# A hybrid SSD and GLA decoder layer: the SSD output kept feature-major, other first loads, and the last norm's shift made on TensorE

## The chip, the cores and the metric

The kernel runs on one core of a Trainium2 chip. TensorE multiplies matrices out of SBUF into PSUM; VectorE (DVE) and ScalarE (ACT) read and write both memories; GpSimd (POOL) works on SBUF alone; loads and stores are issued from the queues of SyncE (SP) and ScalarE. The metric is the device time of one execution in microseconds, less being better.

## The reference

One layer for 256 tokens of width 2048, all in float32:

```
proj = x @ w_in                      # z, xbc, dt, q, k, v, g, lr and two merge gates
xbc  = silu(conv4(xbc))              # gives xs, B, C
y    = ssd(xs, softplus(dt), B, C)   # chunks of 128 tokens, 64 heads of 64, 8 groups, state 128
y    = group_rms_norm((y + D * xs) * silu(z)) * ssd_norm_w    # 8 groups of 512 features
o    = rms_norm(gla(q, k, v, log_sigmoid(lr @ gk_w + gk_b) / 16)) * silu(g)
mix  = (sig(gate_s) * (y @ w_ssd) + sig(gate_g) * (o @ w_gla)) @ w_out
h    = layer_norm(alpha * x + mix)
out  = layer_norm(alpha * h + relu(h @ w_up)^2 @ w_down)
```

Inside a chunk the SSD is a masked product, `y_diag = (C B^T * decay) (x dt)`. For the second chunk a carried-in part is added, `exp(a_cs) * (C prev)`, where `prev` is the state that the first chunk leaves and `a_cs` the running sum of `dt * A`.

## The kernel before

All weights come as one stream of units of 128 x 2048 (1 MB), in the order that `weight_plan` writes out by hand. `Stream` loads each unit on SP's queue into one of three raw buffers and splits it by halves of 1024 columns into a rounded part `whi` (a cast on ScalarE, L139) and a remainder `wlo` (a subtraction on VectorE, L140). Three such halves are kept. Activations are split the same way, so that three products of the fast float32 type stand for one of full precision.

There are two ways to multiply. Form A (`a_unit`, L272 to L288, called by `mm_a`) keeps the activations in the array and moves 512 weight columns: three products (L285 to L287) for each of 16 k-tiles and two token tiles, 96 for a block of 512 features, with tokens on the partitions of the result. Form B (`mm_b`, L245 to L271) keeps the weights in the array and moves the activations: a product of 512 columns (L261) and one of 256 (L264) for each k-tile, 16 such pairs for 128 features, with features on the partitions; a copy (L268) and an addition (L269) then make the sum.

After each half of a unit `run_side` lets a generator go on by a few steps. This is how work that is not the stream of products (scans, norms, the small products of SSD and GLA) gets in between; a planner of the framework then sets the final order on each engine.

The order of stages is: GLA heads 0 to 3, GLA's gates and branch, eight SSD groups, SSD's gates and branch, `w_out`, first norm, `w_up` and `w_down`, last norm. In an SSD group six form-B blocks give xs, B and C with the convolution, then a form-A block gives z, tokens on the partitions. The generator `side_ssd` transposes xs (L670), builds the decayed mask `M` for each chunk, multiplies (L711, features on the partitions), copies, transposes back to token-major (L718), adds the `D` part `yD` and, for the second chunk, the carried-in part (L702 and two passes on VectorE). After z it multiplies, sums squares on ScalarE, takes the power -1/2 on GpSimd for one number a token (`rstd_of`, L328), scales, and transposes again (L740) into the split, feature-major operand of the branch.

At the start ten products of ones (L198) keep TensorE busy, the constants `K` and two small tensors go out on ScalarE's queue, and x and the first weights on SP's. The first side product is `lrT` by `gkw_sb` (L485), with 16 rows. At the end `ln2_last` (L970) norms the second token tile: after the last product VectorE adds, takes statistics, GpSimd takes the power, and VectorE, ScalarE and GpSimd share four blocks of 512 columns.

Of the kernel before, what the change touches and what calls it, by code (L numbers as in the profile page):

```python
# [11 lines left out]
F32 = mybir.dt.float32  # L12
# [25 lines left out]
def weight_plan():  # L38
# [47 lines left out]
class Stream:  # L86
# [26 lines left out]
    def start(self, between):  # L113

        t = self.raw_pool.tile([P, 2048], F32, name="wr", tag="wr")
        for i in range(4):
            q = slice(i * 512, (i + 1) * 512)
            self.nc.sync.dma_start(t[:, q], self.ws[0, :, q])
            between(i)
        self.raws.append(t)  # L120
        self.n_raw = 1
        self._load()
        self._load()
# [48 lines left out]
def hybrid_layer(ctx, tc, ws, xT, x, cst, gkw, dpar, lnp, out):  # L172
# [24 lines left out]
    for _ in range(10):  # L197
        PE.matmul(ps0[:, 0:P], warm, warm, start=True, stop=True)  # L198
# [73 lines left out]
    def a_unit(ps, mat, row, col, u, act, steps=STEPS, units=4):  # L272

        st.expect("A", mat, row + u * 512, col)
        for s in range(2):
            hi, lo = st.half()
            hi = hi.rearrange("p (k c) -> p k c", k=2)
            lo = lo.rearrange("p (k c) -> p k c", k=2)
            for k in range(2):
                kt = u * 4 + s * 2 + k  # L280
                a = act(kt)
                ah, al = a[:, 0], a[:, 1]
                for t in range(2):
                    tt = slice(t * P, (t + 1) * P)
                    pe().matmul(ps[t], ah[:, tt], hi[:, k], start=kt == 0, stop=False)  # L285
                    pe().matmul(ps[t], ah[:, tt], lo[:, k], start=False, stop=False)  # L286
                    pe().matmul(ps[t], al[:, tt], hi[:, k], start=False, stop=kt == 4 * units - 1)  # L287
            run_side(steps)  # L288
# [34 lines left out]

    def rstd_of(pool, ss, scale):
        v = pool.tile([P, 1], F32, name="rv", tag="rv", bufs=2)
        r = pool.tile([P, 1], F32, name="rr", tag="rr", bufs=2)
        V.tensor_scalar(v, ss, scale, EPS, ALU.mult, ALU.add)
        G.tensor_tensor(r, v, nhalf, ALU.pow)  # L328
        return r
# [50 lines left out]
    tokp = cp.tile([P, 6, 64], F32, name="tokp")  # L380

    def side_dt(dtT, pool):
# [33 lines left out]
        S.activation(s2[:, P:T], e[:, P:T], AF.Exp)  # L416
# [3 lines left out]
        for i, src in enumerate((y[:, 0:P], y[:, P:T], e[:, 0:P], e[:, P:T], s2[:, 0:P], s2[:, P:T])):  # L420
            pe().transpose(ps[:, i * 64:(i + 1) * 64], src, ident[0:64, 0:64])
        S.copy(tokp, ps[:, 0:384].rearrange("p (a b) -> p a b", a=6))
# [10 lines left out]
    with tc.tile_pool(name="gla", bufs=1) as gp:  # L433
        ga_scope = ExitStack()
        ga = ga_scope.enter_context(tc.tile_pool(name="gla_in", bufs=1, side="right"))
        gkw_sb = ga.tile([16, 1024], F32, name="gkw_sb")
        lrT = ga.tile([16, T], F32, name="lrT")
# [8 lines left out]
        def load_x(*parts):  # L446
            for i in parts:
                xr[i] = xp.tile([P, 2, T], F32, name="xr", tag="xr", bufs=4)
                nc.sync.dma_start(xr[i], xT[:, 2 * i:2 * i + 2])

        def split_x(i):
            d = xs[:, 2 * i:2 * i + 2]
            S.copy(d[:, :, 0], xr[i])
            V.tensor_tensor(d[:, :, 1], xr[i], d[:, :, 0].bitcast(F32), ALU.subtract)

        def side_x():
            for i in range(2, 8):
                split_x(i)
                if i < 6:
                    load_x(i + 2)  # L460
                yield

        load_x(0)
        st.before[2] = lambda: load_x(2, 3)
        st.start(lambda i: load_x(1) if i == 1 else None)
        split_x(0)
        st.split_first(0)
        st.split_first(1)
# [3 lines left out]
        nc.scalar.dma_start(K, cst)  # L472
        nc.scalar.dma_start(Dbc, dpar.broadcast_to([P, 64]))
        nc.scalar.dma_start(gkw_sb, gkw)
# [100 lines left out]
        for h in range(NH):  # L575
            if h == 0:
                psv, psg = [mtile(), mtile()], [mtile(), mtile()]
                for u in range(4):
                    a_unit(psv, "w_in", 0, C_V, u, xact)
                    a_unit(psg, "w_in", 0, C_G, u, xact)  # L580
                    if u == 1:
                        ps = mm_b("S", "w_in", 0, [xact], bank=stile)
                        S.activation(dtT, ps[0:64], AF.Identity, bias=kcol(K_DTB, 64))
                        S.copy(lrT, ps[64:80])
# [54 lines left out]
    def side_ssd(g, u, sz, yt, ready):  # L639
# [24 lines left out]
        ys = []  # L664
        prev = sp.tile([P, 512], F32, name="prev")
        for c in range(2):
# [7 lines left out]
            yD = sp.tile([P, 8, 64], F32, name="yD", bufs=2)  # L674
            V.tensor_tensor(xdt, psh, hb(tokp[:, c]), ALU.mult)
            if c == 0:
                xw = sp.tile([P, 8, 64], F32, name="xw", tag="xw")
                V.tensor_tensor(xw, psh, hb(tokp[:, 4]), ALU.mult)
            yield
            V.tensor_tensor(yD, psh, hb(Dbc), ALU.mult)  # L680
# [9 lines left out]
            yield  # L690
            for q in range(2):
# [3 lines left out]
            if c == 0:  # L695
                ps = stile()
                pe().matmul(ps, Bt, xw.rearrange("p h e -> p (h e)"), start=True, stop=True)  # L697
                S.copy(prev, ps)
                yield
            else:  # L700
                ps = stile()
                pe().matmul(ps, CT[:, cc], prev, start=True, stop=True)  # L702
                yo = sp.tile([P, 8, 64], F32, name="yo", tag="xw")
                V.tensor_tensor(yo, ps.rearrange("p (h e) -> p h e", h=8), hb(tokp[:, 5]), ALU.mult)
                V.tensor_tensor(yD, yD, yo, ALU.add)
                yield

            py = stile()
            for h in range(8):
                e = h % 2 * 64  # L710
                pe().matmul(py[e:e + 64, h // 2 * P:(h // 2 + 1) * P], xdt[:, h], M[:, h], start=True, stop=True)  # L711
            yield
            yT = sp.tile([P, 512], F32, name="yT", tag="xw")
            S.copy(yT, py)
            yield
            py = stile()
            for i in range(4):
                pe().transpose(py[:, i * P:(i + 1) * P], yT[:, i * P:(i + 1) * P], ident)  # L718
            yield
            yf = yD.rearrange("p h e -> p (h e)")  # L720
            V.tensor_tensor(yf, yf, py, ALU.add)
            ys.append(yf)
# [3 lines left out]
        for c in range(2):  # L726
            y = ys[c]
            V.tensor_tensor(y, y, sz[:, c], ALU.mult)
            ss = sp.tile([P, 1], F32, name="sss", bufs=2)
            S.activation(sz[:, c], y, AF.Square, accum_out=ss)  # L730
            r = rstd_of(sp, ss, 1.0 / 512.0)
            S.activation(y, y, AF.Copy, scale=r)
            yield
        for v2 in range(2):
            ps = stile()
            for j in range(2):
                for c in range(2):
                    f = (v2 * 2 + j) * P
                    o = j * T + c * P
                    pe().transpose(ps[:, o:o + P], ys[c][:, f:f + P], ident)  # L740
            yield
            for j in range(2):
                f = v2 * 2 + j
                w = kcol(K_SN + g * 4 + f)
                pj = ps[:, j * T:(j + 1) * T]
                S.activation(yt[:, f, 0], pj, AF.Copy, scale=w)
                V.scalar_tensor_tensor(yt[:, f, 1], pj, w, yt[:, f, 0].bitcast(F32), ALU.mult, ALU.subtract)
                yield

    ytiles = []  # L750
    for g in range(NG):
# [12 lines left out]
        sz = sp.tile([P, 2, 512], F32, name="sz")  # L764
# [61 lines left out]
    def aggregate(stats):  # L826
        mv = lp.tile([P, 2], F32, name="mv", tag="mv", bufs=2)
        V.bn_aggr(mv, stats)
        r = rstd_of(lp, mv[:, 1:2], 1.0)
        nm = lp.tile([P, 1], F32, name="nm", tag="nm", bufs=2)  # L830
# [139 lines left out]
    def ln2_last():  # L970
        mv, r, nm = aggregate(stats2[:, 1])
        sh = [lq.tile([P, 512], F32, name=f"sh{n}") for n in range(3)]

        def blk(n):
            return (acc[:, 1, n * 512:(n + 1) * 512], gb2[:, 0, n * 512:(n + 1) * 512],
                    gb2[:, 1, n * 512:(n + 1) * 512])

        a0, g0, b0 = blk(0)
        a1, g1, b1 = blk(1)
        a2, g2, b2 = blk(2)  # L980
        a3, g3, b3 = blk(3)
        S.activation(sh[1], g1, AF.Copy, scale=nm)
        S.activation(a3, a3, AF.Identity, scale=r, bias=nm)
        S.activation(a2, a2, AF.Copy, scale=r)
        G.tensor_tensor(sh[1], sh[1], b1, ALU.add)
        G.tensor_tensor(a3, a3, g3, ALU.mult)
        V.scalar_tensor_tensor(sh[0], g0, nm, b0, ALU.mult, ALU.add)
        V.scalar_tensor_tensor(a0, a0, r, sh[0], ALU.mult, ALU.add)
        out_dma(1, 0)
        V.scalar_tensor_tensor(sh[2], g2, nm, b2, ALU.mult, ALU.add)  # L990
        V.tensor_tensor(a2, a2, sh[2], ALU.add)
        out_dma(1, 2)
        V.scalar_tensor_tensor(a1, a1, r, sh[1], ALU.mult, ALU.add)
        out_dma(1, 1)
        V.tensor_tensor(a3, a3, b3, ALU.add)
        out_dma(1, 3)
# [78 lines left out]
```

## Time and profile before

| | |
|---|---|
| median of 3 runs | 2065.91 us (2064.96 to 2067.52) |
| profiled execution | 2071.1 us, its span 2069.4 us |
| TensorE busy | 2052.5 us, 99% |
| VectorE busy | 1272.8 us, 62% |
| ScalarE busy | 1042.0 us, 50% |
| GpSimd busy | 25.5 us, 1% |
| mean granted TensorE clock | 0.995 |
| read from HBM | 391.40 MB, 191 GB/s with what is written |

Busy time says which engine is nearly always occupied, not which wait ends last. The chain goes back from the last instruction and names at each step what released it; windows give the busy time and the granted clock in a stretch. A pass of a full-precision product shows as an instruction of its own, two for each product; a transpose is one.

### The profile page before, as it was taken

To read this page: it belongs to the slowest core of one execution; us is meant where nothing else is said; L and a number is where in the kernel's file an instruction comes from. 1 tells how busy PE (TensorE), PEld (TensorE's weight loads), DVE (VectorE), ACT (ScalarE), POOL (GpSimd) and SP (SyncE) were. 2 spreads that over 40 slices of the span, in tenths; PEclk is the share of its full clock that TensorE was granted. 3 is DMA by queue.
4 is the path that set the end of the run, shared out by engine and by line. 5 is a ranking of instruction groups with operands and counts; after the bars stand their busy time and mean duration, and the time that the engine had idled before them with its cause. 6 is when DMAs were issued, how large, how long until landed. Compare 5 with 4: busy or idle time off the path is not lost.

```text
span 2069.4 us, 25710 instructions
## 1 busy us (share of the span) xinstructions
PE 2052.5 (99%) x10243; PEld 1715.9 (83%) x10243; DVE 1272.8 (62%) x1695; ACT 1042.0 (50%) x1347; POOL 25.5 (1%) x52
## 2 busy tenths in 40 slices
PE   9999999999999999999999999999999999999997
PEld 7888888888888888888888888888888888888886
DVE  5645556445778777777554555686655565565456
ACT  5655545444666666666544443464443443444333
POOL 0000000000000000000000000000000000000000
PEclk9999999999999999999999999999999999999999
DMA  6444455656455554454555556565555555555553
GB/s 249 164 168 168 178 183 214 218 199 223 163 193 194 183 183 177 173 197 167 190 207 198 200 197 224 209 239 185 195 190 190 196 184 198 187 191 195 187 199 122
DMA packets 59321, 397.35 MB, mean 192 GB/s; under 512 B 6736, under 2 KB 6960, under 8 KB 12608
## 3 DMA queue, kind: packets, MB, share of 16 engines
q1 hardware_dynamic: 53568, 374.37, 50.2%
q10 hardware_dynamic: 5632, 21.33, 2.8%
q8 instruction: 80, 1.31, 0.3%
q14 instruction: 41, 0.34, 0.0%
HBM read 391.40 MB, written 4.28 MB: 191 GB/s over the span
## 4 chain that ended last, share of the span: by engine, by line
PE 98%; DVE 1%; DMA 1%; ACT 0%; issue 0%; POOL 0%; DVEq 0%; SPq 0%; POOLq 0%; ACTq 0%
PE mm L261 22%; PE mm L285 19%; PE mm L286 19%; PE mm L287 19%; PE mm L264 11%; PE mm L318 1%; PE sd L711 1%; PE mm L316 1%; PE mm L317 1%; DMA wr<-in_ws_dram 0%; PE sd L718 0%; PE sd L740 0%; PE sd L670 0%; PE sd L697 0%; PE sd L534 0%; PE sd L702 0%
## 5 line engine op out<-in xcount | busy, mean ns | idle before, releaser
L140 DVE TENSOR_TENSOR wlo<-wr,whi 128x1024 fp32r<-128x1024 f32 (+1 forms) x684 | 834.8, 1221 | 660.4 <-ACT whi L139 659.4
L139 ACT CAST whi<-wr 128x1024 fp32r<-128x1024 f32 (+1 forms) x684 | 717.4, 1049 | 887.3 <-PE mm L287 582.1
L261 PE MATMUL mm<-act,whi 128*128 128x512 f32 x1984 | 667.3, 396 | 0.0
L264 PE MATMUL mm<-act,wlo 128*128 128x256 f32 x1984 | 507.4, 280 | 0.0
L261 PEld LDWEIGHTS mm<-act,whi 128*128 128x128 f32 x1984 | 365.8, 188 | 79.2 <-issue 3.4
L264 PEld LDWEIGHTS mm<-act,wlo 128*128 128x128 f32 x1984 | 360.5, 189 | 8.5
L285 PE MATMUL mm<-whi,ys 128*128 128x512 f32 x864 | 336.3, 389 | 0.0
L287 PE MATMUL mm<-whi,ys 128*128 128x512 f32 x864 | 336.2, 389 | 0.0
L286 PE MATMUL mm<-wlo,ys 128*128 128x512 f32 x864 | 336.1, 389 | 0.0
L285 PE MATMUL mm<-whi,act 128*128 128x512 f32 x768 | 312.9, 408 | 0.8 <-ACT whi L139 0.8
L286 PE MATMUL mm<-wlo,act 128*128 128x512 f32 x768 | 301.8, 393 | 1.0 <-DVE wlo L140 1.0
L287 PE MATMUL mm<-whi,act 128*128 128x512 f32 x768 | 301.5, 393 | 0.0
L287 PEld LDWEIGHTS mm<-whi,ys 128*128 128x128 f32 x864 | 162.2, 188 | 33.9
L285 PEld LDWEIGHTS mm<-whi,ys 128*128 128x128 f32 x864 | 162.2, 188 | 33.6
L286 PEld LDWEIGHTS mm<-wlo,ys 128*128 128x128 f32 x864 | 162.2, 188 | 33.5
L285 PEld LDWEIGHTS mm<-whi,act 128*128 128x128 f32 x768 | 145.3, 189 | 37.3 <-issue 6.4
L286 PEld LDWEIGHTS mm<-wlo,act 128*128 128x128 f32 x768 | 145.3, 189 | 34.8 <-issue 2.9
L287 PEld LDWEIGHTS mm<-whi,act 128*128 128x128 f32 x768 | 145.2, 189 | 31.1
L759 DVE SCALAR_TENSOR_TENSOR u<-bsum,K,u 128x255 f32<-128x255 f32 x144 | 68.9, 479 | 26.1 <-ACT u L757 24.9
L269 DVE TENSOR_TENSOR bsum<-mm,bsum 128x256 f32<-128x256 f32 x124 | 51.8, 417 | 12.2 <-ACT bsum L268 12.2
L268 ACT COPY bsum<-mm 128x256 f32<-128x256 f32 x124 | 45.2, 365 | 6.3 <-PE mm L264 6.3
L757 ACT ACTIVATE u<-bsum,K 128x256 f32<-128x256 f32 x48 | 28.9, 601 | 21.8 <-DVE bsum L269 21.8
(230 smaller groups left out, 1246.1 us busy)
## 6 DMA issues: line engine op xcount, KB each, us to landing
wr<-in_ws_dram SPq DMA_DIRECT2D x352, 1024.0 KB, 4.8
abc<-acs_dram ACTq DMA_DIRECT2D x8, 1024.0 KB, 6.7
xr<-in_xT_dram SPq DMA_DIRECT2D x8, 256.0 KB, 6.6
gbias<-gb_dram ACTq DMA_DIRECT2D x8, 256.0 KB, 4.4
mg_dram<-sgr ACTq DMA_DIRECT2D x4, 512.0 KB, 5.9
mgl<-mg_dram ACTq DMA_DIRECT2D x4, 512.0 KB, 3.6
acc<-in_x_dram ACTq DMA_DIRECT2D x2, 1024.0 KB, 7.7
gb<-in_lnp_dram ACTq DMA_DIRECT2D x8, 256.0 KB, 4.6
```

Source lines behind the costliest of these rows:

```text
L139: self.nc.scalar.copy(hi, raw)
L140: self.nc.vector.tensor_tensor(lo, raw, hi.bitcast(F32), ALU.subtract)
L261: PE.matmul(ps, hi[:, k], act(s * 8 + k).rearrange("p s t -> p (s t)"), start=r == 0 and s == 0 and k == 0, stop=False)
L264: PE.matmul(ps[:, T:], lo[:, k], act(s * 8 + k)[:, 0], start=False, stop=r == n - 1 and s == 1 and k == 7)
L268: S.copy(y, ps[:, T:])
L269: V.tensor_tensor(y, ps[:, 0:T], y, ALU.add)
L285: pe().matmul(ps[t], ah[:, tt], hi[:, k], start=kt == 0, stop=False)
L286: pe().matmul(ps[t], ah[:, tt], lo[:, k], start=False, stop=False)
L287: pe().matmul(ps[t], al[:, tt], hi[:, k], start=False, stop=kt == 4 * units - 1)
L316: pe().matmul(ps, ah[:, tt], hi[:, k], start=kt == 0, stop=False)
L757: S.activation(u[:, i], ps, AF.Identity, scale=kcol(K_CW + ft * 4 + 3), bias=kcol(K_CB + ft))
L759: V.scalar_tensor_tensor(u[:, i, j:T], ps[:, 0:T - j], kcol(K_CW + ft * 4 + 3 - j), u[:, i, j:T], ALU.mult, ALU.add)
```

## The change

The block z of each SSD group becomes four form-B blocks of 128 features, so that `silu(z)` has features on the partitions. The SSD output stays feature-major. `yT` takes `D * xs` from the convolved xs and the products from PSUM in one VectorE step for each 128 x 128 piece, with `D` as a column (`Dcol`). The carried-in part is added in PSUM: C is multiplied by `exp(a_cs)` for each head (`abc`), and eight products with `prev` as the array's operand go onto the same PSUM columns. The norm's sum over 512 features is three additions on VectorE and a product with the tile of ones `warm`, which puts each token's sum on all partitions; GpSimd then takes the power of 128 x 256 numbers, and VectorE multiplies. Transposes L718 and L740 are gone.

Besides this: the first loads have other sizes and another order, three warm-up products fewer are made, and the first unit's products with `wlo` come last for each k-tile; the small tensors are loaded behind part 2 of x. `gkw_sb` and `lrT` have 128 partitions of which 112 are zero. In the last norm the shift of three blocks is made in PSUM, `ident` by beta ahead of the statistics and the diagonal of `nm` by gamma behind them, and GpSimd no longer takes part in the blocks.

```diff
-        plan += [("A", "w_in", 512 * i, C_Z + g * 512) for i in range(4)]
+        plan += [("B", "w_in", 0, C_Z + g * 512 + i * P) for i in range(4)]
...
+        for n, cuts in ((0, (0, 512, 1024, 2048)), (1, (0, 1024, 2048))):
+            t = self.raw_pool.tile([P, 2048], F32, name="wr", tag="wr")
+            for a, b in zip(cuts, cuts[1:]):
+                self.nc.sync.dma_start(t[:, a:b], self.ws[n, :, a:b])
+                between(n, a)
+            self.raws.append(t)
...
-    for _ in range(10):
+    for _ in range(7):
...
-        gkw_sb = ga.tile([16, 1024], F32, name="gkw_sb")
-        lrT = ga.tile([16, T], F32, name="lrT")
+        gkw_sb = ga.tile([P, 1024], F32, name="gkw_sb")
+        lrT = ga.tile([P, T], F32, name="lrT")
...
+                if i == 2:
+                    for small, src in ((K, cst), (gkw_sb[0:16], gkw), (Dbc, dpar.broadcast_to([P, 64]))):
+                        G.tensor_copy(small[0:1, 0:1], xr[i][0:1, 0, 0:1])
+                        nc.scalar.dma_start(small, src)
...
+        G.memset(gkw_sb, 0.0)
+        G.memset(lrT, 0.0)
+        nc.scalar.dma_start(xr[0][:, 0], xT[:, 0])
+        def between(n, a):
+            if n == 0 and a == 0:
+                nc.sync.dma_start(xr[0][:, 1], xT[:, 1])
+            elif n == 0 and a == 512:
+                load_x(nc.sync, 1)
+        st.before[3] = lambda: load_x(nc.sync, 2, 3)
+        st.before[4] = lambda: load_x(nc.sync, 4, 5)
+        st.before[5] = lambda: load_x(nc.sync, 6, 7)
...
-            V.tensor_tensor(yD, psh, hb(Dbc), ALU.mult)
...
+                S.activation(abc[:, :, cc], abc[:, :, cc], AF.Exp)
+                V.tensor_tensor(abc[:, :, cc], abc[:, :, cc], CT[:, None, cc].broadcast_to([P, 8, P]), ALU.mult)
...
+            for f in range(4):
+                fc = slice(f * P, (f + 1) * P)
+                for h in (2 * f, 2 * f + 1):
+                    e = slice(h % 2 * 64, h % 2 * 64 + 64)
+                    pe().matmul(py[e, fc], xdt[:, h], M[:, h], start=True, stop=c == 0)
+                if c == 1:
+                    for h in (2 * f, 2 * f + 1):
+                        e = slice(h % 2 * 64, h % 2 * 64 + 64)
+                        pe().matmul(py[e, fc], prev[:, h * 64:(h + 1) * 64], abc[:, h, cc], start=False, stop=True)
+            yield
+            for f in range(4):
+                V.scalar_tensor_tensor(yT[:, f, cc], u[:, f, cc], Dcol[:, g * 4 + f:g * 4 + f + 1],
+                                       py[:, f * P:(f + 1) * P], ALU.mult, ALU.add)
...
+        V.tensor_tensor(yT, yT, sz, ALU.mult)
+        S.activation(sz, yT, AF.Square)
+        yield
+        V.tensor_tensor(sz[:, 0:2], sz[:, 0:2], sz[:, 2:4], ALU.add)
+        V.tensor_tensor(sz[:, 0], sz[:, 0], sz[:, 1], ALU.add)
+        yield
+        yield
+        ps = stile()
+        pe().matmul(ps[:, 0:T], warm, sz[:, 0], start=True, stop=True)
+        v = sz[:, 1]
+        V.tensor_scalar(v, ps[:, 0:T], 1.0 / 512.0, EPS, ALU.mult, ALU.add)
+        G.tensor_tensor(v, v, nhalf.broadcast_to([P, T]), ALU.pow)
+        yield
+        yield
+        V.tensor_tensor(yT, yT, v[:, None, :].broadcast_to([P, 4, T]), ALU.mult)
...
-        ps = mm_a("w_in", 0, C_Z + g * 512, xact)
-        for t in range(2):
-            S.activation(sz[:, t], ps[t], AF.Silu)
+        for i in range(4):
+            ps = mm_b("B", "w_in", C_Z + g * 512 + i * P, [xact])
+            S.activation(sz[:, i], ps, AF.Silu)
...
+        shift = [stile() for n in range(3)]
+        for n in range(3):
+            pe().matmul(shift[n], ident, gb2[:, 1, n * 512:(n + 1) * 512], start=True, stop=False)
+        mv, r, nm = aggregate(
+            stats2[:, 1],
+            lambda: V.tensor_tensor(acc[:, 1, 1536:2048], acc[:, 1, 1536:2048], gb2[:, 0, 1536:2048], ALU.mult))
+        dnm = lq.tile([P, P], F32, name="dnm")
+        S.activation(dnm, ident, AF.Copy, scale=nm)
+        for n in range(3):
+            pe().matmul(shift[n], dnm, gb2[:, 0, n * 512:(n + 1) * 512], start=False, stop=True)
+        sh = lq.tile([P, 512], F32, name="sh")
+        V.scalar_tensor_tensor(sh, gb2[:, 0, 1536:2048], nm, gb2[:, 1, 1536:2048], ALU.mult, ALU.add)
+        for n in (3, 0, 1, 2):
+            a = acc[:, 1, n * 512:(n + 1) * 512]
+            V.scalar_tensor_tensor(a, a, r, sh if n == 3 else shift[n], ALU.mult, ALU.add)
+            out_dma(1, n)
```

## Rows read from the trace of the kernel before

**Rows 1.** The page's chain that ended last, shares of the span by engine.
```profile
PE 98%; DVE 1%; DMA 1%; ACT 0%; issue 0%; POOL 0%; DVEq 0%; SPq 0%; POOLq 0%; ACTq 0%
```
**Rows 2.** Windows, one SSD group: stretch, length, busy time (instructions) by engine, clock, DMA.
```profile
542.60:605.70 63.10, 63.10 (x355) 52.89 (x357) 48.27 (x82) 41.68 (x58) 1.10 (x2) 1.00 0.48 183
```
**Rows 3.** Timeline of TensorE at the start: start, duration, instruction; first and 49th product.
```profile
5.80 1.01 PE L285 MATMUL mm<-whi,act 128*128 128x512 f32 x2
...
20.55 0.39 PE L285 MATMUL mm<-whi,act 128*128 128x512 f32 x1
```
**Rows 4.** Timeline of the tail, from the last product on.
```profile
2056.22 0.39 PE L318 MATMUL mm<-act,ys 128*128 128x512 f32 x1
...
2058.72 0.55 POOL L328 TENSOR_TENSOR rr<-rv,nhalf 128x1 f32<-128x1 f32 x1 [10.33 <-DVE rv L327]
...
2060.16 0.75 DVE L990 SCALAR_TENSOR_TENSOR sh<-gb,nm 128x512 f32<-128x512 f32 x1
...
2060.71 1.32 POOL L985 TENSOR_TENSOR sh<-sh,gb 128x512 f32<-128x512 f32 x1 [1.45 <-ACT sh L982]
2060.82 1.75 DVE L988 SCALAR_TENSOR_TENSOR acc<-acc,rr,sh 128x512 f32<-128x512 f32 x1
...
2064.83 0.68 DVE L995 TENSOR_TENSOR acc<-acc,gb 128x512 f32<-128x512 f32 x1
```
**Rows 5.** Windows around the L485 products; the third last column is the granted clock.
```profile
40.00:44.00 4.00, 4.00 (x16) 2.41 (x15) 2.10 (x4) 3.92 (x9) 0.00 (x0) 1.00 0.07 31
44.00:48.00 4.00, 4.00 (x10) 2.27 (x8) 2.96 (x4) 2.67 (x5) 0.00 (x0) 0.50 0.75 266
...
52.00:56.00 4.00, 4.00 (x10) 3.15 (x10) 0.00 (x0) 2.16 (x5) 0.00 (x0) 0.50 0.02 4
56.00:60.00 4.00, 4.00 (x16) 3.22 (x15) 1.98 (x3) 3.97 (x6) 0.00 (x0) 0.80 0.29 45
```
**Rows 6.** Chain of waits, same stretch: start, time on the chain, engine, tile, line.
```profile
42.54 1.05 PE sd L485 x4
...
48.84 0.43 PE mm L286
```
**Rows 7.** Chain of waits in one SSD group: shares by line, and pieces.
```profile
by line: PE mm L261 35.6%; PE mm L264 18.1%; PE mm L285 11.9%; PE mm L287 11.6%; PE mm L286 11.6%; PE sd L711 3.6%; PE sd L740 1.4%; PE sd L718 1.4%; PE sd L670 1.4%; PE sd L702 1.4%; PE sd L697 1.4%; PE sd L651 1.0%; PE sd L652 0.2%
...
558.62 0.86 PE sd L702 x2
...
562.28 1.02 PE sd L711 x16
563.30 1.12 PE mm L261 x4
...
566.30 0.44 PE sd L718 x4
```
**Rows 8.** Timeline of TensorE, first and last of 68 undisturbed form-B pairs.
```profile
493.43 0.40 PE L261 MATMUL mm<-act,whi 128*128 128x512 f32 x1
...
516.66 0.39 PE L261 MATMUL mm<-act,whi 128*128 128x512 f32 x1
```
**Rows 9.** Groups by line: shapes, count, busy us, mean ns, idle before and releasers.
```profile
L140 DVE TENSOR_TENSOR wlo<-wr,whi 128x1024 fp32r<-128x1024 f32 (+1 forms) x684 | 834.8, 1221 | 660.4 <-ACT whi L139 659.4
L139 ACT CAST whi<-wr 128x1024 fp32r<-128x1024 f32 (+1 forms) x684 | 717.4, 1049 | 887.3 <-PE mm L287 582.1 <-PE mm L261 188.7 <-issue 97.3
...
L269 DVE TENSOR_TENSOR bsum<-mm,bsum 128x256 f32<-128x256 f32 x124 | 51.8, 417 | 12.2 <-ACT bsum L268 12.2
...
L721 DVE TENSOR_TENSOR yD<-yD,sd 128x512 f32<-128x512 f32 x16 | 11.0, 689 | 8.3 <-PE sd L718 8.3
```
**Rows 10.** Cores: span and mean granted clock.
```profile
core 0: 2069.4 us, clock 0.995
```
**Rows 11.** Timeline of ScalarE at the start: casts that waited for weights.
```profile
5.13 0.62 ACT L139 CAST whi<-wr 128x512 fp32r<-128x512 f32 x1 [0.38 <-DMA wr<-in_ws_dram]
...
13.07 1.05 ACT L139 CAST whi<-wr 128x1024 fp32r<-128x1024 f32 x1 [1.78 <-DMA wr<-in_ws_dram]
```

More of the change, by code (lines that the diff above doesn't have):

```diff
@@ L113, in start @@
     def start(self, between):
[L115 to L122, printed above, removed]
+        for n, cuts in ((0, (0, 512, 1024, 2048)), (1, (0, 1024, 2048))):
[4 more added lines that the diff above has]
+            self.raws.append(t)
+        self.n_raw = 2
         self._load()
@@ L282, in a_unit @@
                 ah, al = a[:, 0], a[:, 1]
+                first, last = kt == 0, kt == 4 * units - 1
+                tt = [slice(t * P, (t + 1) * P) for t in range(2)]
+                if st.pos == 1:
+                    for t in range(2):
+                        pe().matmul(ps[t], ah[:, tt[t]], hi[:, k], start=first, stop=False)
+                    for t in range(2):
+                        pe().matmul(ps[t], al[:, tt[t]], hi[:, k], start=False, stop=False)
+                    for t in range(2):
+                        pe().matmul(ps[t], ah[:, tt[t]], lo[:, k], start=False, stop=last)
+                    continue
                 for t in range(2):
[L284 to L287, printed above, removed]
+                    pe().matmul(ps[t], ah[:, tt[t]], hi[:, k], start=first, stop=False)
+                    pe().matmul(ps[t], ah[:, tt[t]], lo[:, k], start=False, stop=False)
+                    pe().matmul(ps[t], al[:, tt[t]], hi[:, k], start=False, stop=last)
             run_side(steps)
@@ L419, in side_dt @@
         ps = stile()
-        for i, src in enumerate((y[:, 0:P], y[:, P:T], e[:, 0:P], e[:, P:T], s2[:, 0:P], s2[:, P:T])):
+        for i, src in enumerate((y[:, 0:P], y[:, P:T], e[:, 0:P], e[:, P:T], s2[:, 0:P])):
             pe().transpose(ps[:, i * 64:(i + 1) * 64], src, ident[0:64, 0:64])
-        S.copy(tokp, ps[:, 0:384].rearrange("p (a b) -> p a b", a=6))
+        S.copy(tokp, ps[:, 0:320].rearrange("p (a b) -> p a b", a=5))
+        Dpair = Dbc.rearrange("p (i two) -> p i two", two=2)
+        G.tensor_copy(Dcol[0:64], Dpair[0:64, :, 0])
+        G.tensor_copy(Dcol[64:P], Dpair[64:P, :, 1])
         yield
@@ L690, in side_ssd @@
             yield
+            if c == 0:
+                ps = stile()
+                pe().matmul(ps, Bt, xw.rearrange("p h e -> p (h e)"), start=True, stop=True)
+                S.copy(prev, ps)
+            else:
+                S.activation(abc[:, :, cc], abc[:, :, cc], AF.Exp)
+                V.tensor_tensor(abc[:, :, cc], abc[:, :, cc], CT[:, None, cc].broadcast_to([P, 8, P]), ALU.mult)
+            yield
             for q in range(2):
@@ L725, in side_ssd @@
             yield "blocked"
[L726 to L747, printed above, removed]
+        V.tensor_tensor(yT, yT, sz, ALU.mult)
[4 more added lines that the diff above has]
+        yield
+        yield
+        ps = stile()
+        pe().matmul(ps[:, 0:T], warm, sz[:, 0], start=True, stop=True)
+        v = sz[:, 1]
+        V.tensor_scalar(v, ps[:, 0:T], 1.0 / 512.0, EPS, ALU.mult, ALU.add)
+        G.tensor_tensor(v, v, nhalf.broadcast_to([P, T]), ALU.pow)
+        yield
+        yield
+        V.tensor_tensor(yT, yT, v[:, None, :].broadcast_to([P, 4, T]), ALU.mult)
+        yield
+        for f in range(4):
+            w = kcol(K_SN + g * 4 + f)
+            S.activation(yt[:, f, 0], yT[:, f], AF.Copy, scale=w)
+            V.scalar_tensor_tensor(yt[:, f, 1], yT[:, f], w, yt[:, f, 0].bitcast(F32), ALU.mult, ALU.subtract)
+            if f % 2:
                 yield
@@ L829, in aggregate @@
         r = rstd_of(lp, mv[:, 1:2], 1.0)
+        with tc.issue_after(var_ins[-1].ins):
+            meanwhile()
         nm = lp.tile([P, 1], F32, name="nm", tag="nm", bufs=2)
```

92 lines of the change are left out of this document (19 added, 73 removed).

## The prediction

> **What bounds the kernel now.** I read the page's chain first: TensorE makes 98% of it [rows 1], so a microsecond counts only where TensorE gains or loses it. Then I looked for the places where that fails. In the SSD stage it never does: one group takes 63.10 us with TensorE busy in all of it, VectorE in 48.27 and ScalarE in 41.68 [rows 2]. At the start the timeline shows the first real product at 5.80 and the 49th at 20.55 [rows 3]; 48 at the 0.231 of a form-A product further on (22.15 us for 96, below) would be 11.1 us, so 3.7 us are waits for loads. At the end the last product starts at 2056.22 and VectorE's last step at 2064.83 [rows 4]: nothing covers that tail. The fourth place is hidden inside a busy TensorE: the granted clock is 1.00 up to 44, 0.50 (1.2 instead of 2.4 GHz) from 44 to 56 and 0.80 in 56 to 60 [rows 5]. TensorE was not idle before it fell; it ran the L485 products, whose operands have 16 partitions, at 1.05 us a pair at the full clock. At the lower level a 512-column product takes 0.43 [rows 6].
>
> **The profiled execution** took 2071.1 us, 1.7 more than its span, and 5.2 more than the median 2065.91. The sum is made against it and carried to the median.
>
> **1. z in form B, eight groups.** The columns are equal: 96 products of 512 before, 64 pairs of 512 and 256 after. In one group's chain the form-A lines hold 35.1% of 63.10, 22.15 us, and the 96 form-B pairs hold 53.7%, 33.88, so 0.353 a pair [rows 7]. 64 pairs are 22.59: 0.44 dearer. From below, the undisturbed stretch at 493.43 to 516.66, 67 pairs, has 0.347 [rows 8]: 0.04 dearer. From above, four more restarts such as the 1.12 instead of 0.93 after a burst [rows 7] make it 1.2.
>
> **2. The SSD output, same groups.** Going: the carried-in product L702 (0.86) and four sets of transposes (L718 and L740, twice each, 0.44 a set): 2.62. Coming: a second burst like L711 for the carried-in part (1.02) and the product with ones, 256 columns of full precision, half of L702: 0.43 [rows 7]. Net 1.17 less. Upper price: a burst's 16 products run 0.064 apart, a transpose of the same 128 columns 0.11; if the interleaving of carried-in and local products ends the overlap of the two column halves, the 32 cost 3.5 instead of 2.04, 1.5 more. From below, the burst could overlap no better than now. With point 1: 0.73 less a group, **5.8 us** over eight (bounds 9.0 less and 12 more).
>
> This costs other engines. VectorE loses eight passes of 128x512 at 0.69 and two tiny ones, 5.8; it gains four sums for z at 0.42, eight steps on 128x128 of PSUM at no more than 0.42, three passes of 1024 columns at 1.22, and 0.69, 0.42 and 0.42 for the norm [rows 9]: 10.2. That makes 52.7 of some 62.4 us, 84%. ScalarE's removed copies, squares and scalings are about what the four extra sums' copies, the wide Exp and Square cost; I take nothing. Both are covered by the weight buffers: a half's cast starts when TensorE frees the buffer (that is the releaser of most casts), the half is due two halves later, 2 x 8 x 0.353 = 5.65 us, and cast and subtraction need 1.05 + 1.22 [rows 9]. So each may come **3.4 us** late for nothing; after that each microsecond is TensorE's. The product with ones waits for two sums on VectorE, with all products queued behind it; the empty turns put around it are worth about a half (2.8 us), more than the 1.1 of the sums.
>
> **3. The power on GpSimd, now 128x256 instead of 128x1.** No row shows it. The one-element form takes 0.55 and a plain 512-column pass 1.32 [rows 4], which gives 0.55 + 0.66 = 1.2 from below; 256 times 0.55 is 141 us from above. It is nearest to the plain pass with the one-element form as its start, so I take 1.2, hidden; it stays hidden while an element costs under 11 ns, four times the plain one. It is not free to VectorE: in the tail L988, 0.75 by itself (L990), took 1.75 beside L985 on GpSimd and ended 0.54 after it; so VectorE stood until GpSimd was done. The subtraction of the weights, two inputs from SBUF like these, is what would stand, and its scaling pass waits for the power as well. The Trainium skill (SBUF — State Buffer, Who interferes with whom) says that "A DVE instruction with two SBUF inputs contends with a GpSimd instruction that reads SBUF", whichever came second waiting for all of the other; the trace agrees. By that rule the whole power falls on VectorE, which is the first rival below.
>
> **4. The 16-partition operands padded to 128.** The low clock lasts 12 + 0.4 x 4 = 13.6 us [rows 5], half of it lost: **6.8 us** less if the wider products hold the clock. Columns and passes stay the same. From below the gain is 0, if zeros count as little as missing rows. I take the full value because the mean clock of 0.995 over 2069.4 us leaves 10.3 us lost [rows 10]: 6.8 here, and the rest falls in the last 8 us, after the products. So nothing else lost the clock, neither the bursts with 64-column operands nor the transposes, and all of those have 128 partitions. The Trainium skill (TensorE: Matmul & The Clock Gate, What's actually happening) sets the clock by how busy the array has lately been. TensorE shows no idle time here, so by busy time alone the padding would do nothing and the sum would be 10.3 less.
>
> **5. First loads.** Before the first cast at 5.13 the constants (350 columns, 0.18 MB), x's part 0 (0.26) and a quarter of a weight unit (0.26) had to land, 0.70 MB; before the cast at 13.07 it was 2.90 MB (all three small loads, two parts of x, two units) [rows 11]: 0.277 MB a us. Now 0.39 MB stand before the first product (1.1 us earlier), and 2.10 before the second unit's first half (2.9 earlier). The second sets the 49th product: **2.9 us** less. Bounds: 0 if x parts 2 and 3, now behind the third unit on SP's queue, are late instead (casts of the next weights would stand behind theirs on ScalarE); 4.8 if all 3.7 of waits go too. The three small loads are issued from ScalarE after x part 2, behind a GpSimd copy; about 1.1 us of issue in front of casts with 3.4 to spare, for constants first used near 40. Three fewer warm-up products: the real ones come before the ten would have ended. The zero fills on GpSimd end before anyone reads.
>
> **6. Tail.** To the power's start, 2058.72, nothing changes [rows 4]. The scaling of the last block (0.69) now stands on VectorE from about 2058.55, so the power waits until 2059.25 and nm is there at 2060.0; then 0.75 for sh and 0.74 for the first block. ScalarE makes the diagonal by about 2060.5; three full-precision products at 0.86 follow, so the blocks end at 2062.25, 2063.05 and 2063.95 instead of 2065.51: **1.6 us** less. The three products with ident go before, 2.6 us from 2056.6, beside VectorE's statistics. Bounds: 2.3 less if the power isn't held up; 0.9 more if the clock falls first (1.72 a product).
>
> Sum: 5.8 + 6.8 + 2.9 + 1.6 = 17.1 less: 2054.0 profiled, **2048.8 us** for the median. With its own bounds this case spans some 2042 to 2055.
>
> **Rivals.**
> *The power holds VectorE* (slower). Place: once a group, beside the weight subtraction. At X us it costs (X - 3.4) x 8. It eats the whole gain at X = 5.5 and is slower by over 0.2% from 6.1; X = 8 gives 2086. For it: the lock is in the trace, and one element at 0.55 is dear. Against: nothing shows how it scales. 0.10 for X between 3.4 and 5.5 (2049 to 2066), 0.14 for more.
> *The padding does nothing* (this part fails to do what it says): 2055.6. For it: TensorE was busy when the clock fell, and the added rows are zeros. Against: point 4. 0.15.
> *The bursts lose their overlap*: 1.5 x 8 = 12 more, 2060.8. Against: local products already alternate the halves. 0.06.
>
> **Chances and range.** The forecast has 0.55. What this kernel's runs can tell from no change is about 0.2%, 4.1 us. Faster (under 2061.8): 0.55 + 0.15 + 0.03 of the third rival + 0.08 of the first = 0.81; same 0.05; slower 0.14. The range 2041 to 2062 reaches from the lower bounds of points 2, 5 and 6 taken in part up to the third rival; outside lie the long powers and a little of the rest, 0.2.
>
> **What would show it.** Right: a group's period of 62.4 with no TensorE gaps; granted clock 1.00 from 40 to 60; the 49th product at 17.7; VectorE's last step about 7.3 after the last product's end. The power's own row on GpSimd decides most: under 3.4 us the subtraction never shows as what TensorE waited for. Wrong: rows of VectorE's subtraction as releasers of TensorE in each group, a pair price above 0.36, or the lower clock again after the L485 products.

## The result, and the profile after

The changed kernel takes 2369.53 us (median of 4, 2368.4 to 2370.62) against 2065.73 of the kernel before on the same chip: 1.1464 times as long, with a 95% interval of 1.1447 to 1.1481. I had forecast 2048.8. The profiled execution spans 2367.7 us.

The page of the kernel after, TensorE's and GpSimd's share, the chain of waits by engine, and the group of the new power:

```profile
PE 2062.5 (87%) x10504; PEld 1738.1 (73%) x10504; DVE 1294.6 (55%) x1760; ACT 1017.6 (43%) x1331; POOL 345.7 (15%) x49
...
PE 83%; POOL 14%; DVE 1%; issue 1%; ACT 0%; DMA 0%; SPq 0%; POOLq 0%; ACTq 0%
...
L765 POOL TENSOR_TENSOR sz<-sz,nhalf 128x256 f32<-128x256 f32 x8 | 329.0, 41122 | 662.2 <-DVE sz L764 662.2
```

TensorE had 98% of the chain before [rows 1]; now GpSimd has 14% of it. The power of 128x256 takes 41.12 us, where I had put 1.2, eight times: 329.0 us. That is near the whole loss of 303.8, but time on GpSimd counts only where TensorE ends up waiting for it. The list of waits says how it reaches TensorE (engine and line that waited, on what, us in total, times, longest):

```profile
DVE yT L768 <- POOL sz L765: 314.8, 8, 41.3
...
PE mm L264 <- DVE wlo L140: 258.6, 7, 37.0
PE mm L295 <- DVE wlo L140: 37.4, 1, 37.4
```

Read upward: TensorE stands 258.6 + 37.4 = 296.0 us for a remainder `wlo` of the weights, and VectorE, which makes `wlo`, stands for the power. VectorE's timeline around the first power, which GpSimd runs from 556.84 to 597.98 (start, duration, instruction, idle before and releaser):

```profile
556.53 0.41 DVE L269 TENSOR_TENSOR bsum<-mm,bsum 128x256 f32<-128x256 f32 x1
556.87 1.67 DVE L140 TENSOR_TENSOR wlo<-wr,whi 128x1024 fp32r<-128x1024 f32 x1
558.46 0.47 DVE L786 SCALAR_TENSOR_TENSOR u<-bsum,K,u 128x255 f32<-128x255 f32 x1
598.01 1.22 DVE L768 TENSOR_TENSOR yT<-yT,sz 128x1024 f32<-128x1024 f32 x1 [39.09 <-POOL sz L765]
599.16 0.48 DVE L786 SCALAR_TENSOR_TENSOR u<-bsum,K,u 128x254 f32<-128x254 f32 x1
599.55 1.22 DVE L140 TENSOR_TENSOR wlo<-wr,whi 128x1024 fp32r<-128x1024 f32 x1
```

One subtraction and one step of the convolution still run beside the power. Then the scaling pass L768, which needs the power's result, is next in VectorE's queue, and the next subtraction stands behind it. TensorE uses up the halves that were split already and stops. The windows show this and what follows it (length, busy time of the engines in the order PE, PEld, DVE, ACT, POOL, granted clock, DMA share, GB/s):

```profile
560.00:596.00 36.00, 3.81 (x22) 3.08 (x21) 0.00 (x0) 0.00 (x0) 36.00 (x1) 0.62 0.00 0
596.00:600.00 4.00, 0.00 (x0) 0.00 (x0) 1.99 (x3) 0.73 (x2) 1.98 (x1) 0.50 0.00 0
600.00:604.00 4.00, 3.18 (x10) 2.79 (x11) 4.00 (x8) 3.72 (x7) 0.00 (x0) 0.50 0.51 178
604.00:608.00 4.00, 4.00 (x18) 3.38 (x18) 3.83 (x9) 2.25 (x4) 0.00 (x0) 0.73 0.62 193
```

TensorE works for the first 3.81 us of the stretch from 560 to 596; after that only GpSimd does. After the idle stretch TensorE comes back at the lower level (0.50) and is at the full one from 608 on, so each group loses a few microseconds more than the wait.

The other parts can be read from the same trace. Around the products of `lrT` the clock is 1.00 in each window, where it was 0.50 [rows 5]:

```profile
44.00:48.00 4.00, 4.00 (x19) 3.11 (x18) 3.80 (x9) 4.00 (x10) 0.00 (x0) 1.00 0.37 156
...
52.00:56.00 4.00, 4.00 (x19) 3.33 (x18) 4.00 (x7) 3.98 (x6) 0.00 (x0) 1.00 0.50 205
```

TensorE's timeline at the start, and at the end TensorE's last product, GpSimd's last power and VectorE's last steps:

```profile
5.65 1.22 PE L287 MATMUL mm<-whi,act 128*128 128x512 f32 x2 [1.17 <-ACT whi L139]
6.67 1.06 PE L289 MATMUL mm<-whi,act 128*128 128x512 f32 x2
...
18.77 0.39 PE L294 MATMUL mm<-whi,act 128*128 128x512 f32 x1
```
```profile
2356.57 0.39 PE L327 MATMUL mm<-act,ys 128*128 128x512 f32 x1
...
2359.07 0.84 POOL L339 TENSOR_TENSOR rr<-rv,nhalf 128x1 f32<-128x1 f32 x1 [10.33 <-DVE rv L338]
...
2361.75 2.46 DVE L1016 SCALAR_TENSOR_TENSOR acc<-acc,rr,sd 128x512 f32<-128x512 f32 x3
```

The 49th product starts at 18.77 (20.55 before [rows 3]; predicted 17.7). The last product of the stream ends at 2356.96, so VectorE's last step ends 7.2 behind it; predicted 7.3, before 8.9 [rows 4].

### The profile page after: what moved, and what is told of

Read it like the earlier page. It is cut to its first block, busy times and chain, and to the rows that moved or that the text cites. A ratio compares the mean times of both kernels' runs of the same rounds, so it can differ in the third digit from the quotient of the medians.

```text
span 2367.7 us, 26328 instructions
## 1 busy us (share of the span) xinstructions
PE 2062.5 (87%) x10504; PEld 1738.1 (73%) x10504; DVE 1294.6 (55%) x1760; ACT 1017.6 (43%) x1331; POOL 345.7 (15%) x49
## 4 chain that ended last, share of the span: by engine, by line
PE 83%; POOL 14%; DVE 1%; issue 1%; ACT 0%; DMA 0%; SPq 0%; POOLq 0%; ACTq 0%
PE mm L261 23%; PE mm L294 14%; PE mm L295 14%; PE mm L296 14%; POOL sz L765 14%; PE mm L264 12%; PE mm L327 1%; PE sd L741 1%; PE mm L325 1%; PE mm L326 1%; DVE wlo L140 0%; DMA wr<-in_ws_dram 0%; PE sd L745 0%; PE sd L704 0%; PE sd L567 0%
## 5 line engine op out<-in xcount | busy, mean ns | idle before, releaser
L264 PE MATMUL mm<-act,wlo 128*128 128x256 f32 x2496 | 650.9, 285 | 258.6 <-DVE wlo L140 258.6
L261 PE MATMUL mm<-act,whi 128*128 128x512 f32 x2496 | 854.5, 401 | 0.0
L264 PEld LDWEIGHTS mm<-act,wlo 128*128 128x128 f32 x2496 | 462.6, 192 | 271.4 <-DVE wlo L140 261.1
L261 PEld LDWEIGHTS mm<-act,whi 128*128 128x128 f32 x2496 | 469.4, 191 | 103.2 <-issue 4.5
L765 POOL TENSOR_TENSOR sz<-sz,nhalf 128x256 f32<-128x256 f32 x8 | 329.0, 41122 | 662.2 <-DVE sz L764 662.2
L295 PE MATMUL mm<-wlo,act 128*128 128x512 f32 x504 | 197.9, 393 | 37.4 <-DVE wlo L140 37.4
L294 PE MATMUL mm<-whi,act 128*128 128x512 f32 x504 | 202.0, 402 | 0.0
L296 PE MATMUL mm<-whi,act 128*128 128x512 f32 x504 | 197.2, 391 | 0.0
L768 DVE TENSOR_TENSOR yT<-yT,sz 128x1024 f32<-128x1024 f32 x8 | 9.8, 1225 | 314.8 <-POOL sz L765 314.8
L772 ACT ACTIVATE ys<-yT,K 128x256 fp32r<-128x256 f32 x32 | 13.7, 496 | 324.3 <-DVE yT L768 324.3
L295 PEld LDWEIGHTS mm<-wlo,act 128*128 128x128 f32 x504 | 95.2, 189 | 58.3 <-DVE wlo L140 37.8
L294 PEld LDWEIGHTS mm<-whi,act 128*128 128x128 f32 x504 | 95.0, 189 | 21.1 <-issue 1.8
L296 PEld LDWEIGHTS mm<-whi,act 128*128 128x128 f32 x504 | 95.1, 189 | 20.0
```

What stands on the lines that cost most here:

```text
L261: PE.matmul(ps, hi[:, k], act(s * 8 + k).rearrange("p s t -> p (s t)"), start=r == 0 and s == 0 and k == 0, stop=False)
L264: PE.matmul(ps[:, T:], lo[:, k], act(s * 8 + k)[:, 0], start=False, stop=r == n - 1 and s == 1 and k == 7)
L294: pe().matmul(ps[t], ah[:, tt[t]], hi[:, k], start=first, stop=False)
L295: pe().matmul(ps[t], ah[:, tt[t]], lo[:, k], start=False, stop=False)
L296: pe().matmul(ps[t], al[:, tt[t]], hi[:, k], start=False, stop=last)
L765: G.tensor_tensor(v, v, nhalf.broadcast_to([P, T]), ALU.pow)
```

## The experiments

Two questions stood open: why a long power, known to me as long only from this trace, stops TensorE, and what the other parts, which were to give 17.1 us together, are worth one by one. For the first there were two theories. *Queue:* the scaling pass waits at the head of VectorE's queue, and the subtractions behind it are late. *Lock,* my own rival: a GpSimd instruction that reads SBUF holds up VectorE's instructions with two SBUF inputs, so the power costs its length wherever its result goes. Ratios are to runs of the kernel before on the same chip.

### e1_narrow: the power of two numbers a partition

```diff
-        pe().matmul(ps[:, 0:T], warm, sz[:, 0], start=True, stop=True)
+        for c in range(2):
+            pe().matmul(ps[:, c:c + 1], sz[:, 0, c * P:(c + 1) * P], warm[:, 0:1], ...)
...
-        G.tensor_tensor(v, v, nhalf.broadcast_to([P, T]), ALU.pow)
+        G.tensor_tensor(r, r, nhalf.broadcast_to([P, 2]), ALU.pow)
...
+        for c in range(2):
+            S.activation(rb[:, c], warm, AF.Copy, scale=r[:, c:c + 1])
...
+        for c in range(2):
+            pe().matmul(ps[:, c * P:(c + 1) * P], rb[:, c], ident, start=True, stop=True)
```

> The norm's power is taken of two numbers for each of 128 tokens (tokens on the partitions, sums by two one-column products), then spread over the features by two products with ident; all else as in the changed kernel. If the long power (41.1 us for 256 columns) is the whole loss, by whichever way it stops VectorE: the power takes about 0.7 us, the eight stalls of 37 us and the low clock behind them go, and the sum of the prediction is left, 2049 to 2056 us. If form B for z or VectorE's load slows the SSD stage by itself: over 2100 us.

Measured: 2058.1 us (2057.86 to 2058.41), ratio 0.9953 (0.9937 to 0.9968). The power of two columns takes 0.69 or 0.70 on GpSimd in six groups, and TensorE waits for `wlo` in all for 0.3 us. With the long power gone, the change is a gain. But it lies 2 us above the range I gave: a group takes 62.75 instead of 63.10 [rows 2]. In the two last groups the power takes 1.51 and 1.57. There it starts inside a subtraction on VectorE and ends 0.54 behind it:

```profile
932.70 1.22 DVE L140 TENSOR_TENSOR wlo<-wr,whi 128x1024 fp32r<-128x1024 f32 x1
932.95 1.51 POOL L766 TENSOR_TENSOR r<-r,nhalf 128x2 f32<-128x2 f32 x1 [62.40 <-DVE bsum L269]
```

### e2_unread: the long powers run, nobody reads them

The scaling pass uses the sum without its power, so this kernel leaves the power out of the result; GpSimd takes two powers of 128x128 in a tile that nothing reads.

```diff
+        w2 = sp.tile([P, P], F32, name="w2")
+        V.tensor_scalar(w2, ps[:, 0:P], 1.0 / 512.0, EPS, ALU.mult, ALU.add)
...
-        G.tensor_tensor(v, v, nhalf.broadcast_to([P, T]), ALU.pow)
+        for _ in range(2):
+            G.tensor_tensor(w2, w2, nhalf.broadcast_to([P, P]), ALU.pow)
```

> Leaves the power out of the output: GpSimd works as long as now (the power of 128 columns twice, 41 us a group, in a tile of its own that nobody reads), and the scaling pass takes the unraised number. Theory of the queue (VectorE stops only because its scaling pass, which waits for the power, stands ahead of the weight subtraction): 2045 to 2060 us, subtractions at 1.2 us during the power. Rival of the lock (a power that reads SBUF keeps VectorE's two-input passes out for its whole length): about 2370 us as now, with subtractions of some 20 us.

Measured: 2086.73 us in one execution, and groups of 62.0 us without a stall, except one: after the last group a cast of the weights on ScalarE waits 37.3 for the last power, and TensorE 31.4 for the cast (probably because a load that ScalarE issues just ahead of the cast gets the memory of that tile; this was not tried). Without that one stop and some 2.7 for the low clock behind it, as behind the other stops (see below), it would be about 2053, an estimate. GpSimd's and VectorE's timelines in one group:

```profile
618.34 41.90 POOL L768 TENSOR_TENSOR w<-w,nhalf 128x128 f32<-128x128 f32 x2 [20.13 <-DVE w L765]
```
```profile
618.84 1.22 DVE L140 TENSOR_TENSOR wlo<-wr,whi 128x1024 fp32r<-128x1024 f32 x1
619.97 1.22 DVE L771 TENSOR_TENSOR yT<-yT,sz 128x1024 f32<-128x1024 f32 x1
```

Two instructions with two SBUF inputs run inside the power in 1.22 us each, their ordinary time [rows 9]. So the lock over the power's whole length falls.

### e3_half: the power of 128 columns

This kernel takes the power of the first 128 tokens only and scales the others by the mean square itself.

```diff
-        G.tensor_tensor(v, v, nhalf.broadcast_to([P, T]), ALU.pow)
+        G.tensor_tensor(v[:, 0:P], v[:, 0:P], nhalf.broadcast_to([P, P]), ALU.pow)
```

> Power of 128 of the 256 columns (the other half of the tokens stays unraised in the output). If the power's time goes by columns, 41.1 becomes 20.6 us, the stall a group falls by the same 20.5, and the time is 2369 - 8 x 20.5 = 2205 us, a little less where the low clock ends sooner. If it has a large fixed part: over 2280 us. If something else than the power is the loss: 2360 us or more.

Measured: 2206.46 us in one execution. The power's group:

```profile
L765 POOL TENSOR_TENSOR sz<-sz,nhalf 128x128 f32<-128x128 f32 x8 | 165.8, 20721 | 659.3 <-DVE sz L764 659.3
```

20.72 for 128 columns and 41.12 for 256: 0.16 us a column, and hardly a start. Half the power gives back 163 us, 20.4 a group.

### e4_later: the scaling pass one group later in the text

```diff
+        late.append((g, yT, v, yt))
...
+    def side_late(n=0):
...
+        g, yT, v, yt = late.pop(0)
+        V.tensor_tensor(yT, yT, v[:, None, :].broadcast_to([P, 4, T]), ALU.mult)
...
+        if g:
+            side.append(side_late())
```

> The full computation with the power of 256 columns; its scaling pass and the split come one group later, behind the next group's power (the unnormed output stays in u, three of which are kept). Theory of the queue: the power, 41 us of a 62 us group, is hidden, and 2050 to 2065 us are left (the last group's may wait some microseconds). Rival of the lock: still a stall of over 30 us in each group, about 2370 us.

Measured: 2368.6 us (2367.85 to 2369.68), ratio 1.1455: no gain. VectorE's timeline shows why; here L776 is the scaling pass:

```profile
556.82 1.67 DVE L140 TENSOR_TENSOR wlo<-wr,whi 128x1024 fp32r<-128x1024 f32 x1
558.41 0.47 DVE L794 SCALAR_TENSOR_TENSOR u<-bsum,K,u 128x255 f32<-128x255 f32 x1
597.97 1.23 DVE L776 TENSOR_TENSOR u<-u 128x1024 f32<-128x1024 f32 x1 [39.08 <-POOL u L765]
```

It stands where it stood, behind its own group's power: the framework's planner sets the order on an engine, and it put the pass back there. So this says nothing on the queue theory; the order had to be forced (e8_held).

### e5_pad, e6_head, e7_tail: one part each on the kernel before

Padding alone, and the first loads and the last norm alone (both as in the diff of the change):

```diff
-        gkw_sb = ga.tile([16, 1024], F32, name="gkw_sb")
-        lrT = ga.tile([16, T], F32, name="lrT")
+        gkw_sb = ga.tile([P, 1024], F32, name="gkw_sb")
+        lrT = ga.tile([P, T], F32, name="lrT")
...
+        G.memset(gkw_sb, 0.0)
+        G.memset(lrT, 0.0)
```

> The kernel before with one part of the change alone: gkw_sb and lrT have 128 partitions, 112 of them zero. If the wider products hold the clock as in the trace of after, 13.6 us at half rate go: granted clock 1.00 from 40 to 60 and 6.8 us less, 2059.2 against some 2066.0. Rival: the one profiled execution of before (2071.1) lay 5 us above its median because its clock fell for longer than in the timed executions; then the trace shows the same 6.8 in its span but the times fall by 2 to 4 us only. If the padding does nothing by itself (and another part of the change held the clock): 2066.0.

> The kernel before with the new first loads alone (cuts of the first units, order of x and the small tensors, seven warm-up products, products with wlo last in the first unit). My prediction had 2.9 us for it: 2063.1. The trace of after had the 49th product 1.8 us earlier, which gives 2064.2. If the padded operands' gain is moved by what the first loads shift, no more than 0.5 either way.

> The kernel before with the new last norm alone (shift of three blocks in PSUM, GpSimd without blocks). Predicted 1.6 us less, 2064.4; the trace of after, last VectorE step 7.2 after the last product instead of 8.9 and the end of the span about 2.1 earlier, gives 2063.9. Rival: the six products at the end cost clock or the memory that sh gave up moves another load: no gain, 2066.

| part | median us | ratio (95%) | gain | predicted |
|---|---|---|---|---|
| kernel before, 27 executions | 2066.12 | 1 | | |
| padding | 2064.6 | 0.9988 (0.9980 to 0.9997) | 1.5 | 6.8 |
| first loads | 2064.98 | 0.9993 (0.9984 to 1.0002) | 1.1 | 2.9 |
| last norm | 2064.26 | 0.9993 (0.9984 to 1.0001) | 1.9 | 1.6 |

The intervals of the last two reach 1, so those two gains are only likely from these runs. Padding is the surprise. The kernel with only the new last norm still has 16 partitions in its products, yet its window and its chain of waits at the same place (L487 is L485 of before) read:

```profile
44.00:48.00 4.00, 4.00 (x16) 2.38 (x15) 3.81 (x7) 3.41 (x8) 0.00 (x0) 1.00 0.59 246
```
```profile
44.59 1.06 PE sd L487 x4
45.65 0.43 PE mm L285
46.08 0.24 PE mm L286
```

The clock stays at 1.00. The low stretch that I read in [rows 5] is not in every execution. In 50 timed ones of the kernel before, run beside these experiments, 9 had a mean granted clock of 0.994 or 0.995 and took 2070.5 to 2073.6 us; the other 41 had 0.996 to 0.998. The execution profiled before the prediction had 0.995 [rows 10]. Of the 22 executions with 16 partitions in e6_head and e7_tail one was low in the same way (0.997 in e7_tail, where the others have 0.999 or 1.000). With padding there was none in 35: the 11 of e5_pad have 0.997 or 0.998, the 24 of e1, e8, e9 and e10, which have the new last norm as well, 0.999 or 1.000. So padding probably does hold the clock, but in the median nothing fell. That the other low executions lost it at the same place is not shown: they have no trace.

What padding saves at the full clock is small. In e5_pad a set of 4 passes (two products) takes 0.86 to 1.05 instead of 1.06, and the product behind it 0.23 instead of 0.43, four times, 1.1 us in all:

```profile
45.12 0.86 PE sd L487 x4
45.98 0.23 PE mm L285
```

### e8_held: the long power is read, but later in VectorE's queue

```diff
-        self.nc.vector.tensor_tensor(lo, raw, hi.bitcast(F32), ALU.subtract)
+        self.sub = self.nc.vector.tensor_tensor(lo, raw, hi.bitcast(F32), ALU.subtract)
...
+        with tc.issue_after(st.sub.ins):
+            V.tensor_tensor(yT, yT, v[:, None, :].broadcast_to([P, 4, T]), ALU.mult)
```

> The kernel after, still with the 41 us powers of groups 0 to 6 and their results read, but the scaling pass is held back in VectorE's queue until the newest weight subtraction of the next group (the run before moved it in the program's text only, and it kept its place in the queue); three buffers for u instead of two; the last group takes the power of 2 numbers a token tile as the narrow kernel does. If a stall is the pass waiting at the head of VectorE's queue, all eight go: no TensorE wait for wlo of over 2 us, groups of about 62.0 us, and 2047 to 2052. If a power that is read costs its 37 us wherever it is read: about 2330. If the powers lengthen VectorE's steps beside them enough to count (1.67 instead of 1.22 for the subtraction): groups of 63 or more, 2055 to 2062.

Measured: 2052.78 us (2052.08 to 2053.25), ratio 0.9933 (0.9921 to 0.9946), 0.8 above the range that I gave. GpSimd's group, its timeline in one SSD group, and VectorE's there (L795 is the scaling pass, of the group before):

```profile
L766 POOL TENSOR_TENSOR u<-u,nhalf 128x256 f32<-128x256 f32 x7 | 287.9, 41123 | 362.6 <-DVE u L765 362.6
```
```profile
618.37 41.13 POOL L766 TENSOR_TENSOR u<-u,nhalf 128x256 f32<-128x256 f32 x1 [20.81 <-DVE u L765]
```
```profile
618.47 1.59 DVE L140 TENSOR_TENSOR wlo<-wr,whi 128x1024 fp32r<-128x1024 f32 x1
619.99 0.47 DVE L813 SCALAR_TENSOR_TENSOR u<-bsum,K,u 128x255 f32<-128x255 f32 x1
620.38 1.21 DVE L795 TENSOR_TENSOR u<-u 128x1024 f32<-128x1024 f32 x1
```

GpSimd spends the same 41.12 us a group (287.9 for seven) and the results are used, but TensorE waits for `wlo` no longer than 0.3 us, and the groups start 62.0 us apart. In these seven groups only the pass's place in the queue differs from e4_later; the eighth group takes the short power of e1_narrow, so its stop is gone for that reason. One subtraction a group takes 1.59 to 1.67 instead of 1.22, the one that starts 0.03 to 0.10 behind the power's start, as in the trace of after; those behind it take 1.21 to 1.23.

### e9_three and e10_held_warm: the parts together, and the warm-up

The first is the kernel before with padding, first loads and last norm; the second is e8_held with one line changed.

```diff
-    for _ in range(7):
+    for _ in range(10):
```

> The kernel before with the padding, the first loads and the last norm of the change, all three, and the SSD output as before. If the three parts add up (1.5, 1.1 and 1.9 less when tried one at a time): 2061.6 against 2066.1, and what the held kernel has beyond that, some 9 us, is the SSD part alone, at 62.02 a group instead of 63.10. If the parts hide one another (the head's gain taken back by a later wait for loads): 2062.5 to 2065. If the padding is worth its predicted 6.8 only together with the others: 2056 to 2058.

> The held kernel with ten warm-up products again instead of seven. With seven, TensorE is idle from 4.48 to 5.62 and its first eight real products run 0.43 apart, as at half rate; with ten in the kernel before the gap is at most 0.45 and after two the products are 0.23 apart. If the idle gap is what slows the first eight: they gain 1.2 to 1.6 us and the median falls from 2052.8 to 2051.2 to 2051.8. If the next unit's loads set the end of this stretch anyhow: the gap appears before the second unit instead and the time stays 2052.8.

e9_three: 2060.87 us (2060.5 to 2061.89), ratio 0.9969 (0.9957 to 0.9981). 5.1 less than the 2065.93 of before: the three add up, to slightly more than the 4.5 of their single runs. e8_held is 8.1 below it, and that is the SSD part with the pass held back.

e10_held_warm: 2052.61 us (2052.24 to 2053.67), ratio 0.9929 against 0.9933 of e8_held: no gain. TensorE's timeline at its start:

```profile
8.04 0.61 PE L291 MATMUL mm<-wlo,act 128*128 128x512 f32 x2
10.47 0.74 PE L287 MATMUL mm<-whi,act 128*128 128x512 f32 x2 [1.82 <-ACT whi L139]
...
18.80 0.39 PE L294 MATMUL mm<-whi,act 128*128 128x512 f32 x1
```

The first products now run 0.23 apart instead of 0.43, and what they gain is given back at 10.47 to a wait for weights. The loads set the 49th product, 18.80 here and 18.34 in e8_held.

## Why the prediction was wrong

**Point 3 failed, in its size.** I took 1.2 us for the power out of bounds of 1.2 and 141; it takes 41.12. I had chosen the end near a plain pass, since a plain 512-column pass was the nearest row in shape. The one-column power, which is the same operation, was the better guide, but it gave only a bound: how much of its 0.55 goes by columns no row then showed. e1_narrow's 0.70 for two leaves 0.15 a column and a fixed 0.40. With the size right, my rival's formula gives (41.1 - 3.4) x 8 = 302 more than the forecast, 2350; measured are 2369.5. The formula's stops were about right: TensorE's waits sum to 296.0. What it lacked is the clock behind each stop: the spans of after and of e8_held differ by 317.3, so 21.3 are not waits, 2.7 a group. That is what some 5.5 us at the lower level cost, an estimate that fits the windows above (0.50 up to 604, 0.73 to 608). The forecast under it was also 4 too low, as the points below show.

**The way it holds VectorE was wrong as well.** My rival had the lock, for all of the power's length; e2_unread and e8_held show subtractions of 1.22 inside a power of 41. I had named the other way in half a sentence (the scaling pass "waits for the power as well") and did not ask what stands behind that pass. The Trainium skill (SBUF — State Buffer, Who interferes with whom) calls the ports that VectorE and GpSimd share an exclusive lock, and lets the instruction that comes second wait for all of the other. The traces agree in part: VectorE's pass beside a plain addition on GpSimd took 1.75 instead of 0.75 [rows 4], and a power that started inside a subtraction waited for its end (1.51 in e1_narrow; point 6 counted on the same in the tail, where the power took 0.84 instead of 0.55). But a 41 us power held a subtraction only up to some 0.5 us behind its own start, an estimate from 1.59 to 1.67 instead of 1.22; the one that started 0.50 behind (e2_unread) took 1.22. The measurement decides; why a long power lets VectorE go so early stays open. The price of the stop is nearly the same either way (37.7 a group by the rival's formula, 37.0 measured), the cure is not: a lock would have needed a shorter power, the queue only another order.

**Point 4: mechanism probably right, size wrong in the median.** The padding seems to hold the clock (none low of 35), and the span of e5_pad's trace, 2063.0, is 6.4 shorter than that of [rows 10]. But 6.8 us was one execution's loss, and I subtracted it from a median in which it was not. The hint stood in my own text: the profiled execution was 5.2 above the median. Measured 1.5.

**Points 1 and 2 were right, and 2 too dear.** z's 64 pairs cost what I took: in e8_held 160 pairs make 91.1% of a group's 62.03, 0.353 each, by the chain's shares:

```profile
by line: PE mm L261 60.5%; PE mm L264 30.6%; PE sd L741 3.3%; PE sd L704 1.4%; PE sd L745 1.4%; PE sd L724 1.4%; PE sd L684 0.9%; PE sd L763 0.7%; PE sd L685 0.2%
```

The bursts L741 and L745 are 4.7% of it, 2.92 us, against two of 1.02 before, 2.04 [rows 7] (the 3.6% there takes in a piece of the next group's). The second burst adds 0.88, not 1.02, and keeps its overlap. A group gains 1.07 instead of 0.73, 8.6 over eight instead of 5.8; what the burst does not explain of this, 0.2 a group, was not followed further. In e1_narrow the two spreading products took 0.44 of it back.

**Point 5** was mis-sized, 1.1 of 2.9. The second unit's first cast came at 12.07 in e6_head, 1.0 earlier than in [rows 11], not 2.9; so the megabytes queued ahead of a load, at one rate for all, did not tell when it lands.

```profile
12.07 1.05 ACT L139 CAST whi<-wr 128x1024 fp32r<-128x1024 f32 x1 [0.32 <-DMA wr<-in_ws_dram]
```

The 49th product of that trace starts at 18.57, 2.0 earlier than in [rows 3]; why the median shows only 1.1 of it stays open. **Point 6** held: 1.9 for 1.6, the last step 7.2 behind the last product where I had said 7.3.

So the sum without the power is 1.5 + 1.1 + 1.9 + 8.6 = 13.1 instead of 17.1, and e8_held, the change with its power out of the way, is 13.3 below the kernel before.

## What to carry to other kernels

An instruction's cost is its place in a queue: before a result from another engine is used, ask how long it takes and what stands behind its reader, and force the order if a planner puts the reader first. Price an unknown operation from rows of the same operation, not from one of the same shape; a row of one size gives a bound, two sizes give the price of a column. Before a loss seen in one profiled execution is subtracted from a median, see whether that execution's time and clock are the median's.

## What was not expected of the hardware

- GpSimd's power goes by columns: 0.55 us for 1, 0.70 for 2, 20.72 for 128, 41.12 for 256, while a plain pass of 512 took 1.32 [rows 4].
- Beside a 41 us power VectorE's passes with two SBUF inputs take their ordinary 1.21 to 1.23, but for the one that starts within 0.1 us behind its start (1.59 to 1.67). A short power that starts inside such a pass waits for its end (1.51 and 1.57 instead of 0.70).
- With 16-partition operands the mean granted clock was low in 9 of 50 executions of the kernel before and in 1 of 22 of e6_head and e7_tail; with 128 partitions in none of 35. In the one low execution with a trace TensorE was busy without a gap [rows 5].
- After TensorE's idle 1.2 us at the start (seven warm-up products) its first products ran 0.43 apart while the column of the granted clock says 1.00. Why the column does not show it stays open.
